# Reordering the end of a state-space loop, one list of modulation sums, and three more block-product tiles in a two-layer decoder trunk

## The chip, the cores and the metric

The kernel runs on one core of a Trainium2 chip. The metric is the device time of one execution in microseconds; the median of several runs is compared. The engines are named as the profile names them: PE is TensorE's matmul and PEld its weight load, DVE is VectorE, ACT ScalarE, POOL GpSimd and SP SyncE, which here issues nearly all DMAs.

## The reference

Two layers on 512 tokens of 1024 channels, all in float32. Each layer is a token mixer and a gated feed-forward network, and each of these four sub-layers is modulated by a conditioning vector `c`.

```python
h = x
for i in range(2):
    shift, scale, gate = split(silu(c) @ ada_w[i, 0] + ada_b[i, 0], 3)
    hn = rmsnorm(h, norm_g[i, 0]) * (1 + scale) + shift
    m = s5_mixer(hn) if i == 0 else fox_mixer(hn)
    h = h + gate * m
    shift, scale, gate = split(silu(c) @ ada_w[i, 1] + ada_b[i, 1], 3)
    hn = rmsnorm(h, norm_g[i, 1]) * (1 + scale) + shift
    h = h + gate * conv_ffn(hn)
return rmsnorm(h, final_g)

def s5_mixer(h):   # 64 groups of 16 channels, each drives a complex diagonal state of 64
    u = h @ w_in
    y = scan(u) + d_skip * u
    y = gelu(y)
    y = y * sigmoid(y @ w_glu)
    return y @ w_out

def conv_ffn(h):   # w_up: 1024 x 5632, w_down: 2816 x 1024
    a, b = split(h @ w_up, 2)
    return (silu(causal_conv3(a) + conv_b) * b) @ w_down
```

`fox_mixer` is causal attention with 16 heads and a forget gate.

## The kernel before

**Products.** Activations lie with channels on the 128 partitions and the 512 tokens along the free dimension. Every large product is done in three passes on a reduced-precision form of float32: each operand is split into a rounded part and a residue (`put_parts`: ScalarE copies `w_hi`, VectorE subtracts to `w_lo`), and hi x hi, hi x lo and lo x hi are accumulated in PSUM (`mms`, L304). A weight tile is 128 x 1024; `raw` is where a DMA of SP lands, `w_hi` and `w_lo` are its parts.

**Networks.** `ffn` goes over 22 inner tiles `f` in groups of 6, 5, 6 and 5. A tile makes the convolution branch and the gate branch of 128 inner channels. After a group is done its rows of `w_down` are worked off one product at a time between the tiles of the next group; the last group's follow behind the loop. A tile whose number stands in `WHOLE_TILES` is two plain products of 8 blocks along the contraction. Any other tile goes through `quarters`, which makes the same two results from 2 x 2 blocks by seven block products (L566) with sums of weight blocks (`sums`, L537) ahead and sums of results (`nm_t`, L537) behind.

**Modulation sums.** Most of the modulation vectors are made by VectorE: a unit of `ada_units` loads a 128 x 1024 row block of `ada_w` into `ada_raw` and multiplies and sums it against `c` in one instruction (L256). 64 units are run. They are generators in a list `bg`; `tick(n)` runs n units at a place in the program, `done` the rest. `SUMS` says how many run after each tile of the first network.

**The state-space layer.** `s5` loops over eight channel tiles `m`. A pass makes the input matrices of tile m+1 (`s5_inputs`: x, the small products `pk` at L979, `ktt`, the transposes and `kt`), the input product of m+2 (L1167), a step of a modulation product (L221), the scan of m (`s5_scan`) and, at its start, the outputs of m-1 (`s5_outputs`: L1053, then the read-out L1061, then the gelu `yg`, written to DRAM as `yd`). `parts(k)` reads a finished tile back (`yt`), copies its rounded part (`a_hi`) on ScalarE and its residue (`a_lo`) on VectorE. With these the first four products of the gate (`glu_head`, L1197) are begun inside and behind the loop: part 0 takes the rounded weights, part 1 their residues. Behind them come the fifth gate product, the sigmoids (L1256), the rest of the gate and `w_out`.

**What sets the order.** The code is recorded and a scheduler orders each engine's instructions; `issue_after(i)` and `behind(...)` put an instruction behind another, and `self.late` holds the one that the next modulation units stand behind. Each engine then works its list strictly in order. PSUM has two pools of four buffers, `mm` and `aux`. `pk` lies in `aux`, which the scan's products and the outputs use as well.

## Time and profile before

| | |
|---|---|
| median of three runs | 1198.78 us |
| the three runs | 1190.84, 1198.78, 1199.16 us |
| the profiled execution | 1197.65 us |
| its span, first to last instruction | 1195.9 us |
| mean granted clock of TensorE | 0.991 |
| busy: PE, DVE, ACT, POOL | 1174.1, 988.7, 592.4, 62.6 us |
| HBM read | 175.53 MB |

The state-space layer takes the first 250 us or so, the first network until about 595, attention until about 840, the second network the rest. Rows of the profile give the engine, the line, the operation, the tile written and the tiles read, the shape and a count; an idle time before a row stands in brackets with what ended it. The granted clock is that which TensorE's throttle allowed, 1.00 being full speed.

### The profile page before, as it was taken

The page shows a single profiled execution, that of the slowest core. Times are in us where ns is not written, and L with a number is a line of the kernel's source. Part 1 is how long each engine was busy: PE and PEld are TensorE (multiplying, and loading weights), DVE is VectorE, ACT ScalarE, POOL GpSimd, SP SyncE. Part 2 cuts the span into 40 slices and gives each one's busy share as a digit, 9 for nine tenths or more (in the row PEclk, how much of TensorE's full clock was granted, in tenths as well). Part 3 has the DMA queues.
Part 4 walks back from the last instruction along what each step waited for, and adds up shares of the span by engine and source line. Part 5 has one row for each costly group of instructions (what it writes and reads, how often), then busy time and mean ns, then how long its engine had stood idle before and what let it go on. Part 6 is the DMA issues. An engine that isn't in the chain of part 4 may idle for free.

```text
span 1195.9 us, 21116 instructions
## 1 busy us (share of the span) xinstructions
PE 1174.1 (98%) x8243; PEld 1026.5 (86%) x8243; DVE 988.7 (83%) x1824; ACT 592.4 (50%) x1069; POOL 62.6 (5%) x114
## 2 busy tenths in 40 slices
PE   7999999999999999999999999999999999999997
PEld 2455687899999999999899788878999999999987
DVE  8899977889888888887776788866899888888855
ACT  2554525346544454453453566554466555555543
POOL 1000000000000000000000443330000000000000
PEclk9999989999999999999999999999999999999999
DMA  9687758822264455554514655523123342343331
GB/s 359 226 256 251 230 167 303 295 92 89 87 204 131 159 174 170 185 184 139 194 36 138 209 185 166 200 76 97 47 75 96 124 124 86 111 124 95 104 88 72
DMA packets 73234, 183.83 MB, mean 154 GB/s; under 512 B 23231, under 2 KB 25503, under 8 KB 72111
## 3 DMA queue, kind: packets, MB, share of 16 engines
q1 hardware_dynamic: 72847, 181.96, 46.6%
q8 instruction: 65, 1.06, 0.4%
q10 hardware_dynamic: 288, 0.52, 0.1%
q14 instruction: 34, 0.28, 0.1%
HBM read 175.53 MB, written 6.92 MB: 153 GB/s over the span
## 4 chain that ended last, share of the span: by engine, by line
PE 86%; DVE 7%; DMA 3%; ACT 2%; issue 1%; POOL 0%; SPq 0%; DVEq 0%; ACTq 0%; POOLq 0%
PE mmp L304 42%; PE mmp L566 15%; PE aux L566 6%; PE mmp L1167 4%; PE mmp L1344 3%; PE mmp L1197 2%; DVE w_lo L288 2%; PE aux L1490 2%; PE aux L1473 1%; PE aux L1061 1%; PE aux L1053 1%; PE mmp L221 1%; PE aux L1443 1%; ACT w_hi L287 1%; DMA raw<-in_w_down 1%
## 5 line engine op out<-in xcount | busy, mean ns | idle before, releaser
L287 ACT ACTIVATE w_hi<-raw 128x1024 fp32r<-128x1024 f32 (+4 forms) x197 | 176.0, 900 | 146.9 <-PE mmp L304 75.5
L288 DVE TENSOR_TENSOR w_lo<-raw,w_hi 128x1024 fp32r<-128x1024 f32 (+4 forms) x197 | 203.4, 1036 | 29.7 <-ACT w_hi L287 25.2
L304 PE MATMUL mmp<-a_hi,w_hi 128*128 128x256 f32 (+1 forms) x600 | 185.9, 311 | 0.0
L304 PE MATMUL mmp<-a_hi,w_lo 128*128 128x256 f32 (+1 forms) x600 | 182.8, 306 | 0.0
L304 PE MATMUL mmp<-a_lo,w_hi 128*128 128x256 f32 (+1 forms) x600 | 182.7, 305 | 0.0
L304 PE MATMUL mmp<-ghi,w_hi 128*128 128x512 f32 (+1 forms) x392 | 143.9, 367 | 0.0
L304 PE MATMUL mmp<-glo,w_hi 128*128 128x512 f32 (+1 forms) x392 | 143.9, 367 | 0.0
L304 PE MATMUL mmp<-ghi,w_lo 128*128 128x512 f32 (+1 forms) x392 | 143.6, 366 | 0.0
L304 PEld LDWEIGHTS mmp<-a_hi,w_hi 128*128 128x128 f32 x600 | 112.4, 188 | 7.6 <-issue 2.6
L304 PEld LDWEIGHTS mmp<-a_hi,w_lo 128*128 128x128 f32 x600 | 112.5, 188 | 6.4
L304 PEld LDWEIGHTS mmp<-a_lo,w_hi 128*128 128x128 f32 x600 | 112.6, 188 | 4.8
L287 ACT ACTIVATE w_hi<-sums 128x1024 fp32r<-128x1024 f32 x68 | 71.6, 1060 | 65.9 <-DVE sums L537 27.4
L566 PE MATMUL mmp<-w_hi 128*128 128x256 f32 x360 | 99.6, 277 | 0.0
L566 PE MATMUL mmp<-w_hi,w_lo 128*128 128x256 f32 x360 | 99.5, 276 | 0.0
L566 PE MATMUL mmp<-w_lo,w_hi 128*128 128x256 f32 x360 | 99.4, 276 | 0.0
L288 DVE TENSOR_TENSOR w_lo<-sums,w_hi 128x1024 fp32r<-128x1024 f32 x68 | 82.4, 1220 | 7.6 <-ACT w_hi L287 6.5
L256 DVE CUSTOM_DVE_ANT_0 ada_raw<-ada_raw,ada_c,rest 128x1024 f32<-128x1024 f32 x64 | 83.7, 1326 | 5.1 <-DMA ada_raw<-in_ada_rows 5.1
L304 PEld LDWEIGHTS mmp<-ghi,w_lo 128*128 128x128 f32 x392 | 73.6, 188 | 12.3
L304 PEld LDWEIGHTS mmp<-ghi,w_hi 128*128 128x128 f32 x392 | 73.6, 188 | 11.2
L304 PEld LDWEIGHTS mmp<-glo,w_hi 128*128 128x128 f32 x392 | 73.6, 188 | 11.1
L378 DVE SCALAR_TENSOR_TENSOR h<-mmp,par,h 128x512 f32<-128x512 f32 (+1 forms) x98 | 62.9, 649 | 23.4 <-PE mmp L304 23.3
L566 PEld LDWEIGHTS mmp<-w_hi 128*128 128x128 f32 x360 | 67.6, 188 | 0.1
(317 smaller groups left out, 2833.0 us busy)
## 6 DMA issues: line engine op xcount, KB each, us to landing
raw<-in_w_up SPq DMA_DIRECT2D x88, 512.0 KB, 3.4
ada_raw<-in_ada_rows SPq DMA_DIRECT2D x64, 512.0 KB, 4.2
raw<-in_ada_w SPq DMA_DIRECT2D x32, 512.0 KB, 5.5
raw<-in_w_down SPq DMA_DIRECT2D x32, 384.0 KB, 3.2
raw<-in_w_down SPq DMA_DIRECT2D x32, 320.0 KB, 3.1
nf<-nfd SPq DMA_DIRECT2D x8, 1152.0 KB, 5.7
raw<-in_fox_qk SPq DMA_DIRECT2D x16, 512.0 KB, 3.2
h<-in_x SPq DMA_DIRECT2D x8, 512.0 KB, 5.5
```

The lines of the kernel that those rows point to most:

```text
L221: self.last_mm = nc.tensor.matmul(ps[32 * qq:32 * qq + 32, :], self.sc32[:, k, :], w[:, q * S:(q + 1) * S], start=(step is steps[0]), stop ...
L256: nc.vector.tensor_tensor_reduce(w, w, self.crow, 1.0, self.ada_b[:, i, m:m + 1], ALU.mult, ALU.add, self.par[i][:, m:m + 1])
L287: nc.scalar.activation(hi, src, AF.Copy)
L288: self.late = (nc.vector.tensor_tensor(lo, src, hi.bitcast(F32), ALU.subtract).ins,)
L304: self.last_mm = self.nc.tensor.matmul(o, wt, xt[:, cols], start=(k == 0 and n == 0), stop=(k == nk - 1 and n == 2),)
L378: self.nc.vector.scalar_tensor_tensor(h, v, self.par[i][:, 16 + m:17 + m], h, op0=ALU.mult, op1=ALU.add,).ins,
L566: self.last_mm = nc.tensor.matmul(o, wt[:, k], xt[:, k], start=(first and k == 0 and n == 0), stop=(k == H - 1 and n == 2), skip_group_che ...
L1053: nc.tensor.matmul(yp[g2][:, k, :], t[:, 2 * k + g2], u[:, g, :], start=(k == 0), stop=False, skip_group_check=True,)
L1167: nc.tensor.matmul(ps, w[m][:, k, :], x[:, k], start=(k == 0), stop=(k == KT - 1))
L1197: nc.tensor.matmul(gps[m], wt, xt[:, k], start=(k == 0 and part == 0 and xt is yhi), stop=(k == KT - 1 and part == 1))
L1344: self.last_mm = nc.tensor.matmul(ps[q, b][:, :n], xt[:, k, tb], wt, start=(k == 0 and i == 0), stop=(k == KT - 1 and i == 2),)
L1490: nc.tensor.matmul(pv[:, c * P:], self.v[:, hp, k, r].rearrange("p t d -> p (t d)"), pp[:, r, c + 3 * k:NB + 3 * k, :].rearrange("p b t -> ...
```

## The change

Six things are changed.

1. Tiles 8, 11, 14, 17 and 20 of the first network go from whole to block products, tiles 10 and 16 the other way: 15 tiles by block products where there were 12.
2. `quarters` writes two of its copies into one tile `both` (a single buffer; one copy negated), and makes the last two sums of a tile in one instruction of 512 columns. This holds for both networks.
3. All modulation units stand in one list from the end of the state-space loop on. `done(left)` runs lists until `left` remain. The ticks are spread otherwise: six units instead of three in the gate products, 23 instead of 32 between the tiles of the first network, four among the first four products of its last group. A unit loads the row of the next one of its list ahead of its own sum.
4. At the end of the state-space loop the residues of the last passes are put behind the last scan, the four residues of gate weights are made together ahead of the modulation units, and these stand behind the last of them. `c` is spread over the partitions at pass 2 instead of after the loop.
5. `pk` moves from PSUM pool `aux` to `mm`.
6. In the parameters of the state-space layer the yield lies ahead of the second step of powers instead of the third.

```diff
-WHOLE_TILES = (0, 1, 2, 3, 4, 8, 11, 14, 17, 20), (0, 1, 2, 3)
-SUMS = (0,) * 6 + (2,) * 16
+WHOLE_TILES = (0, 1, 2, 3, 4, 10, 16), (0, 1, 2, 3)
+SUMS = (0, 0, 0, 0, 1, 1, 1, 1, 1, 1, 2, 1, 1, 2, 1, 1, 2, 1, 1, 2, 1, 2)
...
-    def done(self):
-        while self.bg:
-            assert next(self.bg.pop(0), None) is None
+    def done(self, left=0):
+        while len(self.bg) > left:
+            for _ in self.bg.pop(0):
+                pass
...
     def ada_units(self, i, thirds):
-                w = self.ada.tile([P, D], F32, name="ada_raw", bufs=2)
-                nc.sync.dma_start(w, self.io["ada_rows"][i - ROWS_FROM, m])
+        load = lambda m: nc.sync.dma_start(
+            rows.setdefault(m, self.ada.tile([P, D], F32, name="ada_raw", bufs=2)), self.io["ada_rows"][i - ROWS_FROM, m]
+        )
+        ms, rows = [m for t in thirds for m in range(8 * t, 8 * t + 8)], {}
+        for n, m in enumerate(ms):
+            for a in ms[n:n + 2]:
+                if a not in rows:
+                    load(a)
+            w = rows.pop(m)
...
     def quarters(self, pool, l, f, x, finish):
-        c5 = copy(p5)
+        both = pool.tile([P, 2, N], F32, name="both")
+        copy(p5, both[:, 1])
...
-        c4 = copy(p4)
+        copy(p4, both[:, 0], -1.0)
         times(p1, "s3", "t3", False)
-        sub(ob[:, t2], p1, c5, ALU.add)
-        sub(ob[:, t1], p1, c4)
+        sub(ob.rearrange("p (n t) -> p n t", n=2), p1[:, None, :].to_broadcast([P, 2, N]), both, ALU.add)
...
     def ffn(self, i, l, x, nxt, whole, sums=(), left=0):
-            self.done()
-            down(last, range(KT), tail=TAIL, tail_pool=(pool, 4, TAIL_OFF))
+            self.done(2 * left)
+            down(last, range(KT), tail=TAIL, tail_pool=(pool, 4, TAIL_OFF), ticks=(1,) * left * (KT - TAIL))
+            self.done(left)
...
         for n in (1, 2, 4):
-            if n == 4:
+            if n == 2:
                 yield
...
-        pk = self.aux.tile([P, 2, P], F32, name="aux")
+        pk = self.mm.tile([P, S], F32, name="mmp")[:, :2 * P].rearrange("p (n c) -> p n c", n=2)
...
-            def parts(m):
+            def parts(m, *after):
                 y = self.s5_read_y(pool, m)
                 nc.scalar.activation(yhi[:, m], y, AF.Copy)
-                nc.vector.tensor_tensor(ylo[:, m], y, yhi[:, m].bitcast(F32), ALU.subtract)
+                with self.behind(*after):
+                    nc.vector.tensor_tensor(ylo[:, m], y, yhi[:, m].bitcast(F32), ALU.subtract)
...
                 if m >= KT - 2:
-                    parts(m - 2)
+                    parts(m - 2, *([self.scanned] if m == KT - 1 else []))
+                if m == 2:
+                    self.load_c()
             outputs(KT - 1)
-            self.load_c()
-            self.bg, self.late = [self.ada_units(i, [2])], (self.scanned,)
+            self.bg = [
+                self.ada_units(j, t) for j, t in ((0, [2]), (1, [2]), (2, [0, 1]), (2, [2]), (3, [2]), (3, [0, 1]))
+            ]
             for k in range(KT - 1):
                 if k == KT - 2:
-                    parts(k)
+                    parts(k, self.scanned)
                 glu_head(k, 0)
+            for m in range(HEAD):
+                lo[m] = self.rest([P, KT, P])
+                with tc.issue_after(self.scanned):
+                    self.late = (nc.vector.tensor_tensor(lo[m], raw[m], hi[m].bitcast(F32), ALU.subtract).ins,)
             self.tick(3)
...
-            self.product(self.io["s5_w_glu"], range(HEAD + 1, KT), KT, (yhi, ylo), glu, ticks=1)
+            self.product(self.io["s5_w_glu"], range(HEAD + 1, KT), KT, (yhi, ylo), glu, ticks=(2, 2, 2))
             self.load_x(resid)
-            self.done()
-            self.bg = [self.ada_units(i + 1, [2])]
+            self.done(5)
             after, y = nxt
-            ... tail=2, after=after, ticks=2)
+            ... tail=2, after=after, ticks=(2, 2, 2, 1, 1, 2))
...
-        k.done()
-        k.bg = [k.ada_units(2, [0, 1]), k.ada_units(2, [2]), k.ada_units(3, [2])]
-        x = k.ffn(1, 0, x, k.norm_mod(2), WHOLE_TILES[0], SUMS)
+        k.done(4)
+        x = k.ffn(1, 0, x, k.norm_mod(2), WHOLE_TILES[0], SUMS, 1)
-        k.bg = [k.ada_units(3, [0, 1])]
```

How the list of instructions changes is shown at three places. The first is VectorE at the last scan of the state-space loop, before. `m_1664` and `m_1665` are the rotated inputs of the last scan, the instruction that reads `cf` is the scan, `ua` its states, `a_lo<-yt,a_hi` the residue of a finished tile, `ISA ada_raw` a modulation sum.

```order
L1022 TENSOR_TENSOR m_1664<-aux,s_rot 128x512
L1023 TENSOR_TENSOR m_1665<-aux,s_rot 128x512
L954 TENSOR_TENSOR w_1682<-w_1682,x_1683 128x1024
L1024 TENSOR_TENSOR m_1664<-m_1664,m_1665 128x256
L1186 TENSOR_TENSOR a_lo<-yt,a_hi 128x512
L1025 TENSOR_TENSOR m_1664<-m_1664,m_1665 128x256
L1186 TENSOR_TENSOR a_lo<-yt,a_hi 128x512
L1033 SCALAR_TENSOR_TENSOR m_1665<-cf,m_1664 128x512
L1040 TENSOR_TENSOR ua<-m_1665,s_rot 128x512
L1041 TENSOR_TENSOR ub<-m_1665,s_rot 128x256
L1042 SCALAR_TENSOR_TENSOR ub<-m_1665,s_rot 128x256
L1043 TENSOR_TENSOR ua<-ua,ub 128x512
```

The same place with the change, where the last scan's tiles are `m_1665` and `m_1666`:

```order
L1031 TENSOR_TENSOR m_1665<-aux,s_rot 128x512
L1032 TENSOR_TENSOR m_1666<-aux,s_rot 128x512
L1033 TENSOR_TENSOR m_1665<-m_1665,m_1666 128x256
L1034 TENSOR_TENSOR m_1665<-m_1665,m_1666 128x256
L1042 SCALAR_TENSOR_TENSOR m_1666<-cf,m_1665 128x512
L1049 TENSOR_TENSOR ua<-m_1666,s_rot 128x512
L1050 TENSOR_TENSOR ub<-m_1666,s_rot 128x256
L1051 SCALAR_TENSOR_TENSOR ub<-m_1666,s_rot 128x256
L1052 TENSOR_TENSOR ua<-ua,ub 128x512
L1196 TENSOR_TENSOR a_lo<-yt,a_hi 128x512
L1251 TENSOR_TENSOR w_lo<-raw,w_hi 128x1024 x4
L263 ISA ada_raw,par_96<-ada_raw,ada_c,rest 128x1024
```

No residue stands between the parts of the last scan any more, and the four residues of gate weights come in one piece behind it, ahead of the first modulation sum.

The second place is TensorE between the last read-out and the last pass of the gate's head, before. L1197 are the gate's first four products, L304 into `aux` the fifth, L164 and L169 the columns of the modulation product.

```order
L1197 MATMUL mmp<-a_lo,w_hi 128x512
L1197 MATMUL mmp<-a_hi,w_lo 128x512 x28
L164 MATMUL aux<-rest 128x16
L169 MATMUL aux<-sel,ada_rows 128x4 x4
L304 MATMUL aux<-a_hi,w_hi 128x512
L304 MATMUL aux<-a_lo,w_hi 128x512
L304 MATMUL aux<-a_hi,w_lo 128x512
...
L1197 MATMUL mmp<-a_hi,w_hi 128x512 x4
L1197 MATMUL mmp<-a_lo,w_hi 128x512 x4
L1197 MATMUL mmp<-a_hi,w_lo 128x512 x4
L304 MATMUL aux<-a_hi,w_hi 128x512
```

With the change (L1203 are the gate's first four, L311 the fifth):

```order
L1203 MATMUL mmp<-a_lo,w_hi 128x512
L166 MATMUL aux<-rest 128x16
L171 MATMUL aux<-sel,ada_rows 128x4 x4
L1203 MATMUL mmp<-a_hi,w_hi 128x512 x4
L1203 MATMUL mmp<-a_lo,w_hi 128x512 x4
L1203 MATMUL mmp<-a_hi,w_lo 128x512 x28
...
L1203 MATMUL mmp<-a_hi,w_lo 128x512 x4
L311 MATMUL aux<-a_hi,w_hi 128x512
```

Eleven single L1203 now follow the last read-out, where ten L1197 did; the products of the seventh pass (x4, x4) come behind the modulation columns, and all 24 products of the fifth gate tile come behind the head, where six of them stood ahead of its last pass.

The third place is ScalarE at the sigmoids of the gate, before:

```order
L1256 ACTIVATE nm_t<-mmp 128x512 x2
L287 ACTIVATE w_hi<-raw 128x1024
L287 ACTIVATE zhi<-nm_t 128x512 x2
L1256 ACTIVATE nm_t<-mmp 128x512 x2
L287 ACTIVATE w_hi<-raw 128x1024
```

and with the change:

```order
L1269 ACTIVATE nm_t<-mmp 128x512 x2
L294 ACTIVATE zhi<-nm_t 128x512 x2
L1269 ACTIVATE nm_t<-mmp 128x512 x2
L294 ACTIVATE w_hi<-raw 128x1024
L294 ACTIVATE zhi<-nm_t 128x512 x2
```

The first weight copy of the remaining gate tiles moves from behind two sigmoids to behind four and two copies of `z`.

More of the change, by code (lines that the diff above doesn't have):

```diff
@@ L306, in mms, with product @@
             )
-    def product(self, w, ms, nk, x, evac, head=0, tail=0, after=None, ticks=0, halves=HALVES, tail_pool=(), first=None, step=None, apart=False, ready=(), spare=False):
+    def product(self, w, ms, nk, x, evac, head=0, tail=0, after=None, ticks=(), halves=HALVES, tail_pool=(), first=None, step=None, apart=False, ready=(), spare=False):
         ms = list(ms)
+        ticks = dict(zip(ms, ticks))
         full = slice(0, S)
@@ L334, in product @@
             evac(m, ps, full)
-            self.tick(ticks)
+            self.tick(ticks.get(m, 0))
         if tail:
@@ L569, in times, with copy @@
                     )
-        def copy(o):
-            t = self.tmp.tile([P, N], F32, name="nm_h", bufs=4)
-            nc.scalar.activation(t, o, AF.Copy)
+        def copy(o, t=None, scale=1.0):
+            t = self.tmp.tile([P, N], F32, name="nm_h", bufs=4) if t is None else t
+            nc.scalar.activation(t, o, AF.Copy, scale=scale)
             return t
@@ L1268, in s5 @@
                 glu(m, gps[m], slice(0, S))
[L1269 removed]
+            self.product(self.io["s5_w_glu"], range(HEAD + 1, KT), KT, (yhi, ylo), glu, ticks=(2, 2, 2))
             self.load_x(resid)
[L1271 to L1272 removed]
+            self.done(5)
             after, y = nxt
[L1274 removed]
+            self.product(self.io["s5_w_out"], range(KT), KT, (zhi, zlo), self.add_residual(i, turn=True), tail=2, after=after, ticks=(2, 2, 2, 1, 1, 2))
         return y
@@ L1401, in project @@
                 self.attend(pool, m // 2, qp.pop(m // 2), (hi, lo), nfd)
-        self.product(self.io["fox_qk"], range(NH), KT, x, project, ticks=1, step=self.unit)
+        self.product(self.io["fox_qk"], range(NH), KT, x, project, ticks=(1,) * NH, step=self.unit)
         self.done()
```

29 lines of the change are left out of this document (11 added, 18 removed).

## The prediction

> **What bounds the kernel now.** I read the page's shares first, then a table of stretches, then the waits, then the order of time at the loop's end. The first line answers the coarse question.
>
> ```profile
> PE 1174.1 (98%) x8243; PEld 1026.5 (86%) x8243; DVE 988.7 (83%) x1824; ACT 592.4 (50%) x1069; POOL 62.6 (5%) x114
> ```
>
> TensorE is marked busy nearly always, but a matmul's modelled end reaches over the next one's start, so the share does not say whether it runs at its rate. The count in a stretch does: start, length, then busy time (and count) of each engine, the granted clock, the DMA share.
>
> ```profile
> 100.00:125.00 25.00, 24.71 (x241) 15.27 (x240) 23.86 (x37) 8.65 (x23) 0.00 (x0) 1.00 0.75 243
> 125.00:150.00 25.00, 23.32 (x220) 16.00 (x220) 24.43 (x39) 15.35 (x38) 0.00 (x0) 0.88 0.73 218
> 150.00:175.00 25.00, 25.00 (x185) 21.09 (x184) 18.60 (x28) 8.28 (x23) 0.51 (x6) 0.85 0.48 144
> 175.00:200.00 25.00, 24.14 (x112) 19.78 (x111) 17.73 (x25) 12.59 (x19) 0.00 (x0) 1.00 0.94 337
> 200.00:225.00 25.00, 25.00 (x111) 20.40 (x110) 21.40 (x32) 11.06 (x14) 0.00 (x0) 1.00 0.80 280
> 300.00:325.00 25.00, 25.00 (x223) 25.00 (x222) 22.28 (x33) 13.95 (x21) 0.00 (x0) 1.00 0.30 95
> ...
> 144.00:157.60 13.60, 13.60 (x113) 12.34 (x109) 11.38 (x18) 8.96 (x22) 0.35 (x4) 0.50 0.37 107
> 350.00:550.00 200.00, 200.00 (x1458) 187.97 (x1457) 170.31 (x250) 89.65 (x131) 0.52 (x1) 1.00 0.52 169
> 875.00:925.00 50.00, 50.00 (x422) 49.18 (x422) 49.64 (x70) 29.40 (x46) 0.00 (x0) 1.00 0.25 79
> 950.00:1125.00 175.00, 175.00 (x1259) 163.81 (x1258) 148.78 (x222) 93.94 (x147) 0.00 (x0) 1.00 0.35 108
> ```
>
> From 200 on TensorE issues without a break: 25/223 = 0.112 us for a product of 256 columns (at 300), 25/111 = 0.225 us for 512 (at 200). There time is the count of matmuls. From 100 to 150 it is otherwise: weight loads fill 15 to 16 of 25 us, VectorE 23.9 and 24.4. The state-space loop is VectorE's, and TensorE takes over between 150 and 175, where VectorE falls to 18.6. So two things can shorten the run: fewer matmuls after 190, or an earlier end of VectorE's chain before 170.
>
> The waits of VectorE in that chain, as total, times and longest:
>
> ```profile
> DVE ktt L983 <- PE aux L979: 5.7, 4, 2.8
> DVE a_lo L1186 <- ACT a_hi L1185: 5.4, 2, 4.6
> ```
>
> The longest of the second kind stands between the last scan's rotation and the scan itself:
>
> ```profile
> 142.82 0.25 ACT L991 ACTIVATE kt<-aux 128x128 f32<-128x128 f32 x1
> 142.96 0.66 PE L988 MATMUL aux<-rest,x 128*128 128x128 f32 x4 [1.41 <-ACT w L989]
> ...
> 147.02 3.68 PE L1061 MATMUL aux<-ua,w 64*128 64x63 f32 x32
> ...
> 161.38 2.00 PE L1061 MATMUL aux<-ua,w 64*128 64x63 f32 x32
> ...
> 163.41 0.66 ACT L1067 ACTIVATE yg<-aux 128x256 f32<-128x256 f32 x2 [6.48 <-PE aux L1061]
> ...
> 164.62 0.69 DVE L1186 TENSOR_TENSOR a_lo<-yt,a_hi 128x512 fp32r<-128x512 f32 x1 [4.59 <-ACT a_hi L1185]
> 165.23 0.42 DVE L1025 TENSOR_TENSOR m<-m,m 128x256 f32<-128x256 f32 x1
> ...
> 166.17 1.22 DVE L1033 TENSOR_TENSOR_SCAN m<-cf,m 128x512 f32<-128x512 f32 x1
> ...
> 168.82 0.69 DVE L1043 TENSOR_TENSOR ua<-ua,ub 128x512 f32<-128x512 f32 x1
> ...
> 174.75 6.52 PE L1197 MATMUL mmp<-a_hi,w_lo 128*128 128x512 f32 x28
> ...
> 181.25 1.03 PE L169 MATMUL aux<-sel,ada_rows 128*128 128x4 f32 x8
> ...
> 191.59 0.39 PE L304 MATMUL mmp<-a_hi,w_hi 128*128 128x512 f32 x1
> ```
>
> The read-out of the seventh of eight scans on TensorE (161.38) releases the gelu, behind it in ScalarE's queue stand the copies `a_hi`, and for one of them an `a_lo` holds VectorE for 4.59 us with the last scan queued behind. The scans end at 168.82 + 0.69 = 169.51; the first gate product after the loop's own ones starts at 191.59, 22.1 later, and from there TensorE never pauses.
>
> **The change, part by part.**
>
> *Three more tiles by block products.* Tiles 8, 11, 14, 17 and 20 go from whole to seven products, 10 and 16 back. A whole tile is 2 x 8 x 3 x 2 = 96 products of 256 columns, the other 7 x 4 x 3 = 84. 3 x 12 x 0.112 = **-4.0 us**, if VectorE keeps up. Its rows:
>
> ```profile
> L288 DVE TENSOR_TENSOR w_lo<-sums,w_hi 128x1024 fp32r<-128x1024 f32 x68 | 82.4, 1220 | 7.6 <-ACT w_hi L287 6.5
> L256 DVE CUSTOM_DVE_ANT_0 ada_raw<-ada_raw,ada_c,rest 128x1024 f32<-128x1024 f32 x64 | 83.7, 1326 | 5.1 <-DMA ada_raw<-in_ada_rows 5.1
> ...
> L537 DVE TENSOR_TENSOR sums<-raw 128x512 f32<-128x512 f32 x60 | 39.3, 687 | 20.9 <-DMA raw<-in_w_up 20.8
> L537 DVE TENSOR_TENSOR nm_t<-mmp,nm_h 128x256 f32<-128x256 f32 x90 | 35.3, 418 | 0.0
> ...
> 157.29 0.68 DVE L1022 TENSOR_TENSOR m<-aux,s_rot 128x512 f32<-128x512 f32 x1
> ```
>
> A converted tile adds four sums (2.75), 1.5 more residues (1.8) and three closing sums: two of 0.418 and the merged one, for which the nearest row is a 512-wide read of PSUM, 0.68; in all 1.5. That is 6.1, times three 18.2 us. The merge replaces 2 x 0.418 in the twelve old tiles, -1.9. Of the modulation sums 23 instead of 32 stay between the tiles, 9 x 1.33 = -11.9. Net +4.4 us on some 240: VectorE goes from 170.31/200 = 85% to 87%. It ran 49.64 of 50 us at 875 with the weight loads at 49.18, so fullness alone does not stop TensorE. I take the whole -4.0; bounds 0 and -4.0 for this term, the case beyond is a rival.
>
> *The start.* Six operations of the powers go behind the eight of `a_x`:
>
> ```profile
> 24.08 0.28 DVE L887 TENSOR_TENSOR s_w<-s_pr 128x64 f32<-128x64 f32 x1
> ...
> 25.51 0.16 DVE L174 SCALAR_TENSOR_TENSOR ga<-aux,rest 128x8 f32<-128x8 f32 x1
> 25.71 5.36 DVE L1122 SCALAR_TENSOR_TENSOR a_x<-h,ga,aux 128x512 f32<-128x512 f32 x8
> ...
> 51.50 0.29 DVE L983 TENSOR_TENSOR ktt<-aux,dd 128x128 f32<-128x128 f32 x1 [2.81 <-PE aux L979]
> ```
>
> `a_x` starts 25.51 - 24.08 = 1.4 us earlier, and TensorE's in-order chain behind it. VectorE has the same work until 48.7, so what it gains is 1.4 of its 2.81 wait at 51.5: **-1.4** (bounds 0 and -1.4).
>
> *`pk` in the other PSUM pool.* Two of the loop's later waits for L979 stood right behind a rotation that uses the same pool `aux`. With `pk` in `mm`, TensorE makes it earlier, and in the new order four or more operations lie between `x` and `ktt`. The remaining 5.7 - 2.8 = 2.9 us may all go; in a shared queue something else is late next, so I take **-2.0** (0 to -2.9). What pays for it is `mm`: the four gate accumulators want all four of its buffers while one may still hold the last `pk`. That one is free once ScalarE has copied `kt`, at 142.82 in the profile, ahead of the read-out at 147.02 among which the gate products lie, and those are filler; I cost it at nothing.
>
> *The loop's end.* One residue fewer stands ahead of the last scan (0.69), and the residues for passes 5 and 6 are fenced behind it, so the 4.59 wait has no holder left. **-5.3**, bounds 0 (another operand is late) and -6.1 (all 5.4 of that kind of wait, and the residue). The four `w_lo` that now come together, 4.7 us, delay `a_lo` of pass 6 to about 7.2 us after the scans; TensorE has 3 + 8 products of 0.225, read-out 2.0 and modulation columns, 1.3, ahead of it, 6.8: a wait near 0.5. The read of the last `y` stands in SP's queue behind a gate weight and a modulation row that waits for the first modulation sum, done 6.5 us after the scans. In the profile that read went out 177.59 - 169.51 = 8.1 after; no loss. Summed on TensorE from the scans' end: 2.0 + 1.3 + (11 + 8 + 28 + 12 + 24) x 0.225 + 0.5 = 22.5, as against 22.1 now.
>
> *The first gate tile after that.* ScalarE's order puts its `w_hi` behind four sigmoids and two copies, where two sigmoids stood ahead of it:
>
> ```profile
> 187.06 1.28 ACT L1256 ACT_TABLE_LOAD   x1 [3.21 <-PE mmp L1197]
> ...
> 188.35 1.09 ACT L1256 ACTIVATE nm_t<-mmp 128x512 f32<-128x512 f32 x2
> ...
> 189.32 1.06 ACT L287 ACTIVATE w_hi<-raw 128x1024 fp32r<-128x1024 f32 x1
> 190.27 1.15 ACT L287 ACTIVATE zhi<-nm_t 128x512 fp32r<-128x512 f32 x2
> ```
>
> That is 1.09 + 1.15 later, 2.2, against a filler of 24 products that now stands between the gate's head and this tile (5.4 us) where 18 (4.1) did: **+0.9**; with `w_lo` behind two more residues on VectorE up to +2.2, below nothing not, since nothing of this tile moves forward. I take +1.8. Doubled ticks in the gate (six sums for three, 4.0 us) lie in VectorE's free time, 7.3 of 25 us at 175 and 3.6 at 200; the extra rows, 3 x 0.5 MB, take 4.5 us at the 337 GB/s of the row at 175, and the shares 0.94 and 0.80 leave 6.5 free. The ticks of the last down product (four sums, 5.3 us) meet a VectorE that the moved sums freed. Both at nothing; if that cover is gone, at most their own 4.0 and 5.3.
>
> *Load ahead, and `both`.* All waits for rows are 5.1 us of VectorE, off the path after 190: nothing. The single buffer `both` makes ScalarE's copy in the next tile wait for the closing sum of this one; two sets of 12 products, 2.7 us, lie between, so nothing either, and up to 0.7 a tile if VectorE lags so far.
>
> Sum: the scans end 1.4 + 2.0 + 5.3 = 8.7 earlier, of which I give back 1.5 for waits that the new order makes, an estimate: an eighth of the 11.1 us that the two rows of waits hold. That is -7.2. Then +0.4 and +1.8: -5.0. With -4.0: **-9.0**. The profiled execution took 1197.65 us (span 1195.9 and 1.75 around it), so 1188.65; its own place is 1.1 under the median 1198.78 of the runs shown, whose lowest is 1190.84. I say 1188.6.
>
> **The clock.** In the row at 144 the granted clock is 0.50 for 13.6 us: the read-out at 147.02 took 3.68 us, the one at 161.38 2.00. Thus part of the end's waiting is the clock's. The Trainium skill's page "TensorE: Matmul & The Clock Gate", section "Part 1: The HAM clock gate (the "warmup" mystery)", says the array falls to half after an idle window of about 3.4 us and returns after a busy one. The trace does not quite agree: the gap before 142.96, where the dip begins, is 1.41 us, though TensorE's work was thin. By the page the new order, with eight gate products ahead of that read-out, would keep full clock and end in the second rival's time; by the trace thin work is enough, and the dip returns.
>
> **The rivals.**
> - *The loop's gain is spent after the loop.* TensorE needs its 22 us of products after the last scan, and if those of passes 3 and 4 are late, or a DMA at share 0.8 is, the earlier scan only makes a queue. Then only the block products count: 1197.65 - 4.0 = 1193.6. For it: from 150 to 175 weight loads already fill 21.09 of 25 us. Against: then VectorE's chain would not have set the end, and it idled for it.
> - *The clock stays full* at the loop's end: 13.6 us at half clock cost TensorE at most 6.8, of which 1.7 show in the one read-out (3.68 against 2.00); VectorE covers some of it, and I take 3.7 on top: 1184.9.
> - *The change moves waits without removing them*: the last scan waits for its own rotation instead, and VectorE's sums eat the products: 1197.
> - *Slower: VectorE becomes the bound of the first network.* In runs of five block tiles TensorE needs 84 x 0.112 + 5.4 (528 down products of 0.225 over 22 tiles) = 14.8 us a tile; VectorE 148.78/175 of that, 12.6, and one or two sums, 13.9 to 15.3. It decides where its waits pass 0.9 us a tile; 1.7 us of them over 15 tiles cost 12, and the kernel takes 1200.6. Against: the 875 row.
>
> **How the numbers follow.** Forecast (1185.5 to 1191.5) 0.45; spent after the loop 0.22; full clock 0.18; nothing removed 0.07; slower 0.08. The range that leaves out two in ten runs from 1183.5 to 1197, the first from the full clock with all bounds at their far end, the last up to "nothing removed". One per cent is what a measurement here can tell from no change: under 1186.8 lie the full clock and a quarter of the forecast, 0.30; over 1210.8 only the far end of the slower case, 0.02; within, 0.68.
>
> **What would show it.** Right: 36 fewer products of the up line and no pause of TensorE between 200 and 570; the wait of `a_lo` for `a_hi` under 1 us; that of `ktt` near 1.5 in all; the last scan's end at 161 to 164; the first gate product after the head near 186.5. Wrong: a granted clock under 0.85 over a longer stretch before 175, gaps of TensorE ending on `w_lo` or `nm_t` of the first network, or a gate stage whose DMA share reaches 0.95 with TensorE waiting on a weight.

## The result, and the profile after

The changed kernel took 1201.89 us (median of 15 runs, 1196.29 to 1208.41) beside 1192.14 us of the kernel before (15 runs, 1190.84 to 1199.30): a ratio of 1.0075, interval 1.0056 to 1.0093. It is slower, by some 9 us, where -9.0 was forecast. The profiled execution of the changed kernel took 1203.50 us (span 1201.7). Four runs of three kernels below (only_blocks, only_closing and sums_w_out) took 1675 to 6672 us and are left out of the ratios.

The same stretches of it, with the same columns, and the two new places of half clock that matter now:

```profile
144.00:157.60 13.60, 13.09 (x146) 9.68 (x141) 12.07 (x20) 9.15 (x22) 0.34 (x4) 1.00 0.57 183
150.00:175.00 25.00, 24.96 (x221) 21.36 (x222) 21.50 (x32) 11.03 (x26) 0.51 (x6) 1.00 0.64 201
175.00:200.00 25.00, 23.78 (x104) 19.05 (x103) 18.62 (x26) 12.96 (x18) 0.00 (x0) 1.00 0.83 304
350.00:550.00 200.00, 199.24 (x1433) 186.31 (x1432) 174.18 (x250) 99.67 (x151) 0.00 (x0) 1.00 0.46 147
249.60:252.90 3.30, 3.30 (x18) 3.30 (x17) 1.63 (x10) 0.00 (x0) 0.00 (x0) 0.50 0.43 171
597.80:601.00 3.20, 3.20 (x17) 3.20 (x17) 2.13 (x12) 0.42 (x1) 0.00 (x0) 0.50 0.01 3
```

The half clock at 144 is gone, as the better case had it, but it stands at two new places, 249.6 and 597.8, and the short one near the start, 3.4 us from 41.6 before, is now 6.8 us from 51.6. Each of the two follows a wait of TensorE that the kernel before did not have in that size. The waits of the changed kernel (total, times, longest), and behind them the last two of the kernel before:

```profile
DVE a_lo L1196 <- ACT a_hi L1194: 2.5, 3, 1.4
DVE ktt L992 <- PE mmp L988: 3.4, 6, 0.8
PE mmp L574 <- ACT nm_h L581: 3.7, 6, 1.3
PE aux L403 <- DVE ssq L373: 3.6, 2, 2.1
```

```profile
PE mmp L566 <- ACT nm_h L573: 0.3, 1, 0.3
PE aux L395 <- DVE ssq L365: 0.3, 1, 0.3
```

The two waits that the forecast removed shrank, though not as far as it said (`a_lo` from 5.4 to 2.5, where under 1 was forecast, `ktt` from 5.7 to 3.4, where 1.5 was). The two below grew from 0.3 us each: TensorE waits for the row statistics `ssq` at the end of the state-space layer's output product and of the first network, and for the second copy `nm_h` within block tiles. The first, in order of time:

```profile
237.38 1.28 DVE L263 CUSTOM_DVE_ANT_0 ada_raw<-ada_raw,ada_c,rest 128x1024 f32<-128x1024 f32 x1 [1.81 <-DMA ada_raw<-in_ada_rows]
...
243.10 1.27 DVE L263 CUSTOM_DVE_ANT_0 ada_raw<-ada_raw,ada_c,rest 128x1024 f32<-128x1024 f32 x1
...
244.91 1.28 DVE L263 CUSTOM_DVE_ANT_0 ada_raw<-ada_raw,ada_c,rest 128x1024 f32<-128x1024 f32 x1
...
247.64 0.41 DVE L373 TENSOR_TENSOR ssq<-ssq,nm_t 128x256 f32<-128x256 f32 x1
248.11 0.61 PE L403 MATMUL aux<-ones,ssq 128*128 128x1 f32 x4 [2.15 <-DVE ssq L373]
...
595.43 0.61 PE L403 MATMUL aux<-ones,ssq 128*128 128x1 f32 x4 [1.46 <-DVE ssq L373]
```

Modulation sums, one of them after 1.81 us of waiting for its row, stand in VectorE's queue up to the tail; `ssq` is late, TensorE waits 2.15 us, and 1.4 us later its clock is halved. The last line is the second wait, at the end of the first network. There the kernels without the new list of sums wait too, 0 to 1.3 us in 12 profiles, but none of these has half clock behind it; with the list it is 1.5 to 2.7 us in six, with half clock behind it in five.

By stage, in us. The second column is another profile of the unchanged kernel (before_again, below), whose clock fell for 3.4 us at 144 instead of 13.6:

| stage | before, the forecast's profile | before, second profile | after |
|---|---|---|---|
| start to the first gate product after the head | 191.59 | 187.34 | 188.44 |
| to the first product of `s5_w_out` | 16.32 | 16.32 | 17.27 |
| `s5_w_out`, first to last product | 45.99 | 45.75 | 50.71 |
| first network, first to last product | 347.23 | 347.77 | 348.25 |
| attention | 244.24 | 244.24 | 243.86 |
| second network, first to last product | 339.67 | 340.73 | 341.94 |
| span | 1195.9 | 1193.0 | 1201.7 |

Against the second profile the output product is the largest loss, 5.0 of 8.7 us. The network, for which -4.0 was forecast, took no less.

### The profile page after: what moved, and what is told of

It is laid out like the page before. It is cut to its first block, busy times and chain, and to the rows that moved or that the text cites. A ratio compares the mean times of both kernels' runs of the same rounds, so it can differ in the third digit from the quotient of the medians.

```text
span 1201.7 us, 21110 instructions
## 1 busy us (share of the span) xinstructions
PE 1171.8 (98%) x8207; PEld 1022.2 (85%) x8207; DVE 1002.4 (83%) x1821; ACT 601.2 (50%) x1087; POOL 62.6 (5%) x114
## 4 chain that ended last, share of the span: by engine, by line
PE 68%; DVE 14%; DMA 10%; issue 4%; ACT 2%; POOL 0%; SPq 0%; DVEq 0%; ACTq 0%; POOLq 0%
PE mmp L311 33%; PE mmp L574 12%; PE aux L574 5%; PE mmp L1176 4%; PE mmp L1356 3%; DVE w_lo L295 3%; DMA ada_raw<-in_ada_rows 3%; DMA raw<-in_w_up 2%; DVE ada_raw L263 2%; PE aux L1502 2%; DVE sums L545 2%; PE aux L1485 1%; ACT w_hi L294 1%; PE aux L1062 1%; PE aux L1070 1%
## 5 line engine op out<-in xcount | busy, mean ns | idle before, releaser
L311 PE MATMUL mmp<-a_hi,w_hi 128*128 128x256 f32 (+1 forms) x504 | 159.1, 318 | 0.7 <-ACT w_hi L294 0.7
L311 PE MATMUL mmp<-a_hi,w_lo 128*128 128x256 f32 (+1 forms) x504 | 156.5, 311 | 0.5 <-DVE w_lo L295 0.5
L311 PE MATMUL mmp<-a_lo,w_hi 128*128 128x256 f32 (+1 forms) x504 | 156.5, 311 | 0.0
L311 PE MATMUL mmp<-ghi,w_hi 128*128 128x512 f32 (+1 forms) x392 | 144.7, 369 | 0.0
L311 PE MATMUL mmp<-glo,w_hi 128*128 128x512 f32 (+1 forms) x392 | 144.7, 369 | 0.0
L311 PE MATMUL mmp<-ghi,w_lo 128*128 128x512 f32 (+1 forms) x392 | 144.4, 368 | 0.0
L574 PE MATMUL mmp<-w_hi 128*128 128x256 f32 x396 | 110.1, 278 | 3.7 <-ACT nm_h L581 3.7
L574 PE MATMUL mmp<-w_hi,w_lo 128*128 128x256 f32 x396 | 109.4, 276 | 0.0
L574 PE MATMUL mmp<-w_lo,w_hi 128*128 128x256 f32 x396 | 109.3, 276 | 0.0
L311 PEld LDWEIGHTS mmp<-a_hi,w_hi 128*128 128x128 f32 x504 | 94.2, 188 | 8.6 <-issue 2.6
L311 PEld LDWEIGHTS mmp<-a_hi,w_lo 128*128 128x128 f32 x504 | 94.5, 188 | 7.4 <-DVE w_lo L295 1.0
L311 PEld LDWEIGHTS mmp<-a_lo,w_hi 128*128 128x128 f32 x504 | 94.7, 188 | 4.8 <-DVE a_lo L457 0.2
L295 DVE TENSOR_TENSOR w_lo<-sums,w_hi 128x1024 fp32r<-128x1024 f32 x74 | 89.7, 1220 | 8.9 <-ACT w_hi L294 7.3
L311 PEld LDWEIGHTS mmp<-ghi,w_lo 128*128 128x128 f32 x392 | 74.3, 190 | 12.3
L311 PEld LDWEIGHTS mmp<-ghi,w_hi 128*128 128x128 f32 x392 | 74.4, 190 | 11.2
L311 PEld LDWEIGHTS mmp<-glo,w_hi 128*128 128x128 f32 x392 | 74.4, 190 | 11.1
```

What stands on the lines that cost most here:

```text
L295: self.late = (nc.vector.tensor_tensor(lo, src, hi.bitcast(F32), ALU.subtract).ins,)
L311: self.last_mm = self.nc.tensor.matmul(o, wt, xt[:, cols], start=(k == 0 and n == 0), stop=(k == nk - 1 and n == 2),)
L574: self.last_mm = nc.tensor.matmul(o, wt[:, k], xt[:, k], start=(first and k == 0 and n == 0), stop=(k == H - 1 and n == 2), skip_group_che ...
```

## The experiments

Ratios are to the kernel before on the same chip, with 95% intervals. S is the theory that the moved modulation sums hold up the statistics, M that the merged closing sum makes TensorE wait, B that the forecast's base was a disturbed execution, V that VectorE binds the block tiles. Two more come in below: L, that the earlier loads of rows hold other transfers back, and R, that the transfers of the added rows make the statistics late.

### The four parts singly

**only_blocks**

```diff
-WHOLE_TILES = (0, 1, 2, 3, 4, 8, 11, 14, 17, 20), (0, 1, 2, 3)
+WHOLE_TILES = (0, 1, 2, 3, 4, 10, 16), (0, 1, 2, 3)
```

> The kernel before with the new table of whole tiles alone (19 instead of 16 tiles of the first network by seven products... in words: three more), nothing else changed. Three theories of the lost time: S, the modulation sums that were moved into the last product of the state-space layer and into the last down product hold up VectorE ahead of the row statistics, TensorE waits there and its clock halves; M, the merged closing sum makes TensorE wait within block tiles; B, the forecast of the loop was summed from an execution with 13.6 us of half clock, and without that the loop's edits bring little. None of them touches this part: all three expect the 36 products' -4.0 us. A fourth, V, that VectorE binds in runs of block tiles with two sums each, expects -1 to +4.

(The counts in that text should read 15 instead of 12.) Measured 1.0015 (0.9995 to 1.0035), +1.8 us: the -4.0 is missing with nothing else changed.

**only_closing**: `quarters` as in the changed kernel.

```diff
-        c5 = copy(p5)
+        both = pool.tile([P, 2, N], F32, name="both")
+        copy(p5, both[:, 1])
...
-        sub(ob[:, t2], p1, c5, ALU.add)
-        sub(ob[:, t1], p1, c4)
+        sub(ob.rearrange("p (n t) -> p n t", n=2), p1[:, None, :].to_broadcast([P, 2, N]), both, ALU.add)
```

> The kernel before with the merged closing sum and its single buffer alone. M expects +2 to +5 us: in the changed kernel TensorE waits six times for the second copy (3.7 us by its row of waits), and some of it in each network. S, B and V expect 0 (within 1 us), V even a gain of a few tenths, as VectorE has 0.2 us less in each block tile.

Measured 1.0005 (0.9988 to 1.0022). Its profile has TensorE waiting 2.0 us for copies, and its second network took 341.52 us; but kernels that leave that network as it was took 339.61 to 341.40. M is not borne out as a cost that can be measured.

**only_loop**: the powers' `yield` at n = 2, `pk` in `mm`, and the loop's end, all as in the change.

> The kernel before with the three edits of the state-space loop alone: the powers later, pk in the other PSUM pool, the loop's end reordered. The forecast had -5.0 us at the first gate tile for these. B expects -2 to +2 against the usual run of the kernel before, with no stretch of half clock near 144; S and M have no word on it and would leave the forecast's -5.

Measured 0.9993 (0.9977 to 1.0009), -0.8 us: B's value. The first gate product starts at 186.91.

**only_sums**: `ada_units`, `SUMS`, `done`, the list and all ticks as in the change.

> The kernel before with the one list of modulation sums, its new ticks and the load ahead alone; tiles, closing sums and loop as before. S expects +6 to +9 us: 4.7 us in the last product of the state-space layer and 3 at the end of the first network's last down product, with waits of 1.5 to 2.5 us for the row statistics and half clock for about 3.4 us behind each. M and B expect 0; V expects 0 to -2 as 9 sums leave the tiles.

Measured 1.0067 (1.0039 to 1.0095), +8.0 us. Its output product took 50.35 us, with half clock from 247.3 to 250.7 and, behind the end of the first network, from 595.5 to 598.9:

```profile
PE aux L403 <- DVE ssq L373: 4.7, 2, 3.0
```

The four ratios add up to +0.80%, the change's own is +0.75%. So the sums carry nearly all of it.

### The sums, from the other side

**after_old_sums**: the changed kernel, but `ada_units`, `SUMS`, the lists and ticks of the kernel before.

> The changed kernel with the lists, ticks and loads of the modulation sums as in the kernel before (three more block tiles, the merged closing sum and the loop's edits stay). If the sums' new places are the cause (S), the parts found singly add up: +1.8, +0.6 and -0.8 us, so +1 to +3 us against the kernel before, some 6 to 8 less than the changed kernel's +8.9, its last product of the state-space layer takes 45 to 47 us and no half clock follows it. If it is an interaction of the other three parts, +5 or more remain.

Measured 1.0012 (0.9997 to 1.0026); the output product takes 45.71 us, and there is no half clock after 60 us but at the very end. Taking the sums' new places out of the changed kernel gives back 7.5 us. In this one profile the first network took 344.91 us, 2.3 less than before: with the old sums and `both`, part of what the block tiles save does show. Whether `both` is what lets it show was not run singly.

### Which property of the sums

**ahead_only**: `ada_units` loads a row ahead; nothing else.

> The kernel before with the load of a row ahead of the sum before it, alone. S and V: 0 (within 1.5 us). L, that the early loads keep SP's queue and the weights late: +2 to +4 us, with the last product of the state-space layer above 48 us.

Measured 1.0014 (0.9991 to 1.0037); the output product 45.71 us. L, that the early loads themselves block the weights, is not what happens in that product. But its first product comes 17.26 us after the gate's, where kernels without the load ahead take 16.32; so the 0.9 us that the changed kernel loses there belong to the load ahead, which the forecast had at nothing.

**sums_w_out**, from only_sums:

```diff
-... after=after, ticks=(2, 2, 2, 1, 1, 2))
+... after=after, ticks=(2, 2, 2, 2))
```

> The kernel of the one list of sums alone (only_sums), but the last product of the state-space layer gives out two sums behind each of its first four tiles as the kernel before does, in place of 2, 2, 2, 1, 1, 2 over six; the two sums left over go to two whole tiles of the first network. If the sums behind the fifth and sixth tile are what holds the statistics up (S), that product takes 46 to 47.5 us in place of 50.4, TensorE's wait for ssq there is under 0.7 us, no half clock follows, and the kernel is 3 to 4 us shorter than only_sums. If the earlier loading of rows holds back other transfers instead (L), it stays at 50 us.

Measured 1.0034 (1.0004 to 1.0064), 4 us under only_sums by the ratios, as S has it, though the two intervals overlap. The profiled execution ran at a mean granted clock of 0.943, so its stage times are not used; the wait for `ssq` was still 1.8 us in it, with half clock behind it, which S does not explain.

**sums_last**, from only_sums: `down(last, ...)` without ticks, the six sums in the network's tiles.

> The kernel of the one list of sums alone (only_sums), but no sums in the last down product of the first network: its four and the two behind it go to the network's tiles. S: the wait of TensorE for ssq at 592 (1.93 us) falls to the 0.5 to 1.5 us that kernels with no sums there show, the half clock at 595 goes, and the kernel is 2 to 3.5 us shorter than only_sums. The rival, that sums in tiles cost as much as sums there (V), gives 0.

Measured 1.0059 (1.0035 to 1.0082), within the interval of only_sums; TensorE waits 1.81 us for `ssq` ahead of 602.61 all the same, with half clock behind it, although VectorE's last sum starts at 587.89. So sums within that last product are not what makes `ssq` late there.

**sums_short**, from only_sums, leaves VectorE's work out and keeps the loads:

```diff
+                n = 8 if i == 1 or (i == 2 and m < 3) else D
                 nc.vector.tensor_tensor_reduce(
-                    w, w, self.crow, 1.0, ...
+                    w[:, :n], w[:, :n], self.crow[:, :n], 1.0, ...
```

> The kernel of the one list of sums alone (only_sums) with the ten sums that stand in the last product of the state-space layer, and one ahead of it, cut to 8 of their 1024 columns; their rows are still loaded in full, so what is left out is VectorE's work alone. If VectorE's time for the sums holds the statistics up, that product takes 46 to 47 us (50.4 in only_sums) and the wait for ssq is under 0.7 us. If it is the wait for the rows, which hold VectorE's queue, it stays above 48.5 us.

The cut reached the three sums ahead of the product and the first eight of its ten; the last two stayed whole. Measured 1.0073 (1.0056 to 1.0090), the product 51.08 us: nothing gained, which speaks against S except that the last two sums still stood there. Two more kernels settle that.

**sums_short_all**: `m < 5` in that line.

> As sums_short, with the last two sums of that product cut to 8 columns as well (in sums_short they stood whole ahead of the last ssq); all rows are loaded. S: the product falls to 46 to 47.5 us. R: it stays above 49, with VectorE waiting for rows and weights instead.

**sums_no_rows**, from only_sums: five rows are not loaded, their sums read `self.crow` in place of a row.

```diff
-                if a not in rows:
+                if a not in rows and (i, a) not in ((1, 16), (1, 18), (1, 20), (1, 22), (2, 0)):
                     load(a)
+            u = rows.get(m, self.crow)
...
-                    w, w, self.crow, 1.0, ...
+                    w, u, self.crow, 1.0, ...
```

> The kernel of the one list of sums alone (only_sums) with five of the 21 rows up to the end of the state-space layer left out (their sums read another tile of the same size, so VectorE's work stays whole): as many bytes as the kernel before moves there. If the rows' bytes set the pace of the last product, where the DMA engines are 0.81 to 0.89 busy (R), it falls from 50.4 to 46 to 48 us and the wait for ssq from 3.0 to under 1 us. If the sums' own time on VectorE does (S), it stays above 49.

The stretch 203 to 240 and TensorE's waits for `ssq`, first without the five rows (one wait, at the end of the first network), then with all rows and short sums, and VectorE's waits of the latter in the stage:

```profile
203.00:240.00 37.00, 37.00 (x184) 31.44 (x183) 34.28 (x56) 13.47 (x17) 0.00 (x0) 1.00 0.72 241
...
PE aux L404 <- DVE ssq L374: 1.5, 1, 1.5
```

```profile
203.00:240.00 37.00, 37.00 (x185) 31.53 (x184) 20.60 (x54) 12.13 (x15) 0.00 (x0) 1.00 0.85 296
...
PE aux L404 <- DVE ssq L374: 4.6, 2, 2.7
...
DVE ada_raw L264 <- DMA ada_raw<-in_ada_rows: 8.1, 7, 2.5
DVE w_lo L296 <- ACT w_hi L295: 6.6, 6, 2.2
```

With VectorE 34.28 of 37 us busy but fewer bytes, the output product took 45.49 us, with no half clock behind it. With VectorE at 20.60 and all bytes it took 50.52 us, and the half clock stands from 242.9 to 249.7. Up to 240 TensorE issued as many products in both (184 and 185); the 5.0 us between them come behind that, from the wait and the half clock. This decides for R: **the rows' transfers, not VectorE's time**, make `ssq` late. VectorE waits for rows (8.1 us) and for the rounded parts of weights (6.6), in order, and the statistics stand at the end of that queue. Whether the rows cost by their bytes or by their place in SP's queue was not separated. In times: sums_no_rows 1.0029 (1.0005 to 1.0054), sums_short_all 1.0043 (1.0023 to 1.0064), the latter under only_sums (intervals overlap) although its stage is no shorter; why stays open. What makes `ssq` late at the end of the first network was not separated.

### The block tiles

**blocks_light**, from only_blocks: `SUMS = (0,) * 6 + (1,) * 16`; eight sums in the later value products of attention, eight at `ticks=2` in its output product.

> The kernel before with the new table of whole tiles, and only 16 modulation sums in the first network's tiles, one a tile from the seventh on; the other 16 stand in the attention layer (8 behind the later value products, 8 behind the head of its output product). V, that two sums ahead of a block tile's residues delay w_hi and with it the second copy, so that the products saved are waited away: here the saving shows, 36 x 0.112 = 4.0 us less than before in the first network (343 us from its first product to its last, as against 347.2 and 348.7 in only_blocks), and the kernel is 2 to 5 us faster than before. Against V: the network stays at 347 or above, the kernel within 1 us of before.

The network took 344.35 us, 2.9 less than before, but the kernel 1.0075 (1.0046 to 1.0105): the displaced sums cost more than four times that, 4.2 us in the value and attention part and 9.0 in the output product and what follows. TensorE waited there, and its clock was halved from 664.1 to 667.5, 824.6 to 831.4 and 848.5 to 855.3:

```profile
PE aux L425 <- DVE rs_y L416: 2.5, 1, 2.5
PE mmp L304 <- DVE h L378: 1.8, 1, 1.8
```

**blocks_short**, from only_blocks: the 32 sums of the network cut to 8 columns, as above.

> The kernel with three more block tiles alone (only_blocks) with the 32 sums in the first network's tiles cut to 8 of their 1024 columns; rows still loaded, so VectorE has 32 x 1.2 = 38 us less there. V: TensorE's waits for the second copy go, and the network takes 343 us from its first product to its last, 4.0 under the 347.2 of the kernel before. Against V: above 346.

Measured 342.99 us for the network: the full 4 us in this profile, as V has it. The kernel: 0.9989 (0.9972 to 1.0005), so over ten runs only 1.3 us of it (at most 3.3) are seen. The same stretch of only_blocks and of blocks_short:

```profile
350.00:550.00 200.00, 197.65 (x1402) 184.44 (x1401) 181.60 (x274) 96.78 (x148) 0.52 (x1) 0.99 0.51 169
```

```profile
350.00:550.00 200.00, 200.00 (x1440) 187.27 (x1439) 159.58 (x280) 98.94 (x150) 0.52 (x1) 1.00 0.50 171
```

At 181.60 of 200 us VectorE has 18 us left; where it stopped TensorE, it did so by its order. In only_blocks, at the one long pause, VectorE and then ScalarE:

```profile
500.36 1.28 DVE L256 CUSTOM_DVE_ANT_0 ada_raw<-ada_raw,ada_c,rest 128x1024 f32<-128x1024 f32 x1
501.56 1.28 DVE L256 CUSTOM_DVE_ANT_0 ada_raw<-ada_raw,ada_c,rest 128x1024 f32<-128x1024 f32 x1
502.76 0.95 DVE L288 TENSOR_TENSOR w_lo<-raw,w_hi 128x768 fp32r<-128x768 f32 x1
...
504.57 0.68 DVE L537 TENSOR_TENSOR sums<-sums,raw 128x512 f32<-128x512 f32 x1
```

```profile
505.35 1.06 ACT L287 ACTIVATE w_hi<-sums 128x1024 fp32r<-128x1024 f32 x1 [3.28 <-DVE sums L537]
506.31 0.37 ACT L573 ACTIVATE nm_h<-mmp 128x256 f32<-128x256 f32 x1
```

Two modulation sums stand ahead of the next tile's `sums`; ScalarE's `w_hi` waits 3.28 us for those, and behind it in ScalarE's queue stands the copy `nm_h` that frees the accumulator of the tile that TensorE is in. TensorE waited 2.29 us there, and the clock was halved from 507.0 to 510.4.

**blocks_split**, from only_blocks: of a tile's two sums one ahead of the down products.

```diff
+                    s = sums[f] if f < len(sums) else 0
+                    self.tick(s // 2)
                     if q:
                         down(...)
-                    self.tick(sums[f] if f < len(sums) else 0)
+                    self.tick(s - s // 2)
```

> The kernel with three more block tiles alone (only_blocks), but of the two sums of a tile one is put ahead of the down products and one behind them, so that no residue of the next tile waits behind two. If two sums in a row are what delays the second copy (V): the network takes 343.5 to 346 us (348.7 in only_blocks, 347.2 before), -1 to -3 us against the kernel before. If it is VectorE's total in those tiles: as only_blocks, +1 to +3.

Measured 1.0001 (0.9981 to 1.0021), the network 347.50 us, with other waits (1.8 us for `w_lo`) in place of that one. Two sums in a row are thus one way in which it shows; that VectorE's total is the rest is what is left by exclusion, not shown by a run of its own. **loop_blocks_split** adds the loop's edits:

> The kernel before with the three loop edits, the new table of whole tiles and the split of a tile's sums of blocks_split; sums, loads and closing sums stay. The loop's single run was at -0.8 us; with V right this one is 2 to 4 us faster than the kernel before, else -1 to +2.

Measured 0.9996 (0.9980 to 1.0012), the network 346.61 us. No version faster than the kernel before was found.

### The loop

**before_again**: the kernel before, unchanged.

> The kernel before, unchanged, for a second profile. Its profiled execution that the forecast was summed from had half clock from 144.0 to 157.6. B: where that stretch is missing, the scans end near 163.1, the wait of a_lo for a_hi is under 1 us without any edit, and the first gate tile starts near 185.6. If the wait belongs to the order of the work, as the forecast had it, some 4 us of it stand here too.

The half clock lasts 3.4 us here, the wait falls to 1.2, and the last scan ends at 164.61 + 0.69 = 165.30, 4.2 earlier than in the forecast's profile (169.51):

```profile
143.50:146.90 3.40, 3.40 (x39) 2.95 (x39) 2.69 (x4) 2.94 (x8) 0.00 (x0) 0.50 0.49 138
...
164.61 0.69 DVE L1043 TENSOR_TENSOR ua<-ua,ub 128x512 f32<-128x512 f32 x1
...
DVE a_lo L1186 <- ACT a_hi L1185: 1.2, 1, 1.2
```

In ahead_only and only_blocks, with the same loop and no half clock at all there, it ends at 163.13 and 163.21: earlier than the changed kernel's 163.62. All 13 usable profiles with the old loop fall in line: four with 13.65 us of half clock there have a longest wait of 4.1 to 4.6 us and the last scan's end at 169.1 to 170.9, two with 3.4 us have 1.2 to 1.4 and 165.3 to 166.1, seven with none have 0.4 to 1.3 and 162.4 to 163.6. So all but about 1 us of the 4.59 was the clock's, not the order's.

**start_pk**: the powers' `yield` and `pk` alone.

> The kernel before with the powers later and pk in the other PSUM pool; the loop's end stays. The single run of the three loop edits showed the first gate tile 1.3 us later than kernels with the old end (186.9 against 185.6) and no stretch of half clock near 144. If the later gate tile comes from the new loop's end, this kernel has it at 185.6 or before and keeps TensorE busy at 141, so no half clock there: -1 to -3 us against the median of the kernel before, faster than the three edits together. If pk's place costs it, it is at 186.5 or later and the kernel is not faster.

Measured 1.0016 (1.0005 to 1.0027): not faster. Its gate tile starts at 185.81 and TensorE is busy at 141, as was hoped; but a wait of 2.1 us for `x` appears near 51, as in the changed kernel, and half clock from 51.4 to 54.8, which sets in during it:

```profile
52.21 1.08 PE L988 MATMUL mmp<-x,s_cd 128*32 128x128 f32 x16 [2.06 <-DVE x L963]
```

None of the five profiles with the new start and `pk` shows half clock between 140 and 160, and four of them show it from 51 on; of the 13 with the old loop, six show it near 144 and none at 51. The thin stretch was moved from one place to another.

## Why the prediction was wrong, step by step

- **The base** failed first. The sum was made against an execution with 13.6 us of half clock at the place where the largest term, -5.3, was read. Over the 125 runs of the kernel before that stand beside the experiments, the time follows (by a straight line through them) 1189.7 us + 954 us x (1 - granted clock), with a mean of 1193.7 at 0.9957: the profiled 1197.65 at 0.991 was some 4 us above the usual. The prediction had the row (0.50 for 13.6 us) and the line "part of the end's waiting is the clock's", but priced this as a rival on top, not as a deduction from its own term.
- **The loop's order of events** was right in direction: `a_lo` and `ktt` wait less, and the last scan of that profile moves from 169.51 to 163.62 (-5.9; -7.2 forecast). Against an undisturbed execution it is +0.4. The span from the scans' end to the gate tile, 22.1 before, was forecast at 24.3 and is 24.8. With the loop alone -0.8 us is left of -5.0; the start and `pk`, forecast at -3.4, are +1.9 by themselves (start_pk).
- **The doubled ticks in the gate, costed at nothing,** are the step that turned the sign: only_sums alone is +8.0, and without the sums' new places the change is +1.4. Three extra rows were priced at 4.5 us of transfer in 6.5 us of free DMA time. But five rows more, not three, lie ahead of the network (21 sums for 16), the two in the output product went unpriced, and 5 x 0.524 MB at the 287 GB/s that only_sums moves from 203 to 240 are 9.1 us, in stages whose DMA engines were already 0.94 and 0.80 busy in the prediction's rows. Sums_no_rows and sums_short_all show that VectorE's time, for which its free time was named as cover, was not what counted in the output product.
- **The first network**: VectorE's share was forecast at 87% and is 174.18/200 = 87%; TensorE's -4.0 did not follow. That "fullness alone does not stop TensorE" was argued from a row without modulation sums; with them the order of two queues stops it. By blocks_short the 4.0 us is there when VectorE has 80% (159.58/200), by only_blocks it is not at 91%. In the changed kernel 1.46 us of waiting for `ssq` and 1.7 for the half clock behind it come on top; without these its network would take some 345 us, an estimate by 348.25 - 1.46 - 1.7, which is near the 344.91 of after_old_sums. About half of the -4.0 was there, then, and was spent at the network's end.
- **The last down product at nothing, at most 5.3**: the wait and the clock make 3.2 us, but 0.9 of the wait stands in the second profile of the kernel before as well, and sums_last, without sums there, has both. **`both`** at nothing stands, within 2 us.
- **The rivals**: the slower one (0.08) named VectorE in the block tiles, which is part of why the saved products brought nothing; the loss beyond that lies with the rows and the statistics. The first rival did say that a DMA at share 0.8 may be late, but only as a reason why the loop's gain is spent.
- **The clock**: the changed kernel's 15 runs have a mean granted clock of 0.9925 against 0.9957; at 954 us per unit that is 3.1 of the 8.6 us between the means. The other 5.5 are then waiting, by this line and not by a run of its own.

## What to carry to other kernels

Look up the granted clock of the one profile before taking a wait from it: here most of a wait read inside a stretch of half clock was not the program's. Work that is moved takes its transfers along; price them too, as bytes over the stage's rate for a first estimate, for every stage that the work lands in, and ask who stands behind the waiting instruction. And a queue at 87 to 91% can stall an engine through a second in-order queue long before it is full, so ask what a block of side work stands ahead of, not only how much of it there is.

## What the runs showed of the hardware

Half clock comes in whole steps of 3.413 us on a grid: in the changed kernel its edges at 51.6, 58.4, 249.5, 253.0, 597.7 and 601.1 lie 2, 58, 59, 160 and 161 steps from the first. I divided each profile by its own grid and counted the columns of the matmuls in each step (0.112 us for 256). From 60 to 1180 us the 18 usable profiles have 35 steps worth under 0.33 of their time; 33 were followed by half clock, all but two near 62, and a step over 0.40 never was. From 20 to 55 us the count does not tell: 15 of 44 such steps were followed, and why is open. So from 60 us on the step need not be idle, and whether one pause costs 3.4 us of half clock or nothing depends on where the grid falls: the same wait of 1.41 us, ended at 144.33 in only_closing and at 142.87 in only_blocks, was followed by it in the first (step worth 0.23) and not in the second (0.37). The Trainium skill's page "TensorE: Matmul & The Clock Gate", section "Part 1: The HAM clock gate (the "warmup" mystery)", tells of a free-running activity window of that length; the runs agree on the length, and show that from 60 us on work for less than a third of a window was too little.
